# Weighting the first half's attention groups at the operand loads of the out-projection, in a hybrid decoder layer on one core

## The chip, the core and the metric

The kernel runs on one core of a Trainium2 chip. The metric is the device time of one execution in microseconds (us), lower is better. Engines are named as in the profile: PE (TensorE matmul), PEld (its weight load), DVE (VectorE), ACT (ScalarE), POOL (GpSimd), SP (SyncE). In this kernel POOL does hardly more than issue DMAs, and SP does nothing else. Each engine takes its own instructions in order; semaphores hold one back until what it reads is there.

## The reference

One layer over 2048 tokens of width 1024, in float32. Three mixers run side by side on slices of one projection; the concatenation of their outputs goes through an out-projection, and an MLP follows. What the change touches is the end of the attention mixer: three groups of two heads each give an output o and a log-sum-exp, and a softmax over the groups weights the outputs.

```python
h = rmsnorm(x, norm1_g)
z = h @ w_in                          # q|k|v, conv a|gate, LRU gate|x
for g, (window, dilation) in enumerate(((128, 1), (512, 4), (2048, 16))):
    o, lse = dilated_window_attention(q_g, k_g, v_g, ...)   # 2 heads of 64
alpha = softmax(stack(lse), axis=groups)
y_attn = o * alpha[..., None]         # 6 heads = 384 channels
mix = concat([y_attn, conv_module(...), recurrent_mixer(...)])
x = x + mix @ w_out
x = x + relu(rmsnorm(x) @ w_up) ** 2 @ w_down
return rmsnorm(x, final_g)
```

## The kernel before

Channels lie on partitions, tokens along the free axis. The 2048 tokens are worked in two halves of 1024 (h = 0, 1), each in two blocks of 512 (m = 0, 1). A matmul's operands are split into a rounded high part and a low rest, and each product is three matmuls (high·high, high·low, low·high), so every operand costs one ACT copy (high) and one DVE subtraction (low): `split` (L242, L243) and `halves` (L907, L908).

The stages: `inproj(0)`; `inproj(1)` with the first half's mixers between its steps; then for each half the out-projection, the up product and the down product, with the second half's mixers spread through the first half's stages by `tick`. A scheduler orders the instructions of the first part by priority and readiness: `mixers(0)` is recorded with a raised priority and so lands among the instructions of `inproj(1)`. Its parts are attention, the convolution, the recurrent mixer (`lru_mixer`, three passes t = 0, 1, 2) and `combine`.

In `inproj`, one group of 48 matmuls takes 10.9 us into two of four PSUM banks (`mm`); DVE empties them (L388, L390, L393) while PE fills the other two. Weights come by SP into five `raw` tiles (L251) and are split by L242 and L243 some groups ahead.

A pass of `lru_mixer` loads x (`wide<-lscr`, L542) and gate weights (`mr<-gates_w`, L543), runs four steps of a short convolution on DVE (L548, then L552 three times), splits the result (L242 and L243 into `wr`), and multiplies it on PE by the gate weights into bank `cb` (L564 to L566). ACT applies the sigmoid (L567), and DVE and ACT go on with L569, L573 to L580, the scan (L582) and L586; L588 stores to `mscr`. PE's gate matmuls stand among those of `inproj` in one order, so PE waits at L564 or L565 if `wr` is late.

`combine(h)` gets per-token maxima and sums of each group from `sscr` (L802, to `m`), forms the three weights (L808 to L823, small DVE operations and one ACT exponential), and stores them to `wscr` (L827). Then for each of six tiles (block b, group g) it loads the weights back, each row repeated on 64 partitions (L841, two DMAs of 128 KB), loads the group's output from `oscr` (L843), multiplies (L834, 128x512) and stores to `mscr` (L850, L854). For h = 0 all its DMAs go through SP, for h = 1 through POOL.

The out-projection reads eight 128-channel tiles per block from `mscr`: `act_load` (L922) loads some of them into the lower halves of `rounded` tiles, `act_split` (L924) splits them. `MIX_ORDER = [3, 4, 5, 6, 7, 0, 1, 2]` puts attention's three tiles last (n = 5, 6, 7), loaded by one DMA. For the first half `out_first` brings in block 1 during the last groups of `inproj(1)`, `out_second` block 0 afterwards. The matmuls are L948 to L950, 24 to a group of one bank; groups 0 to 3 read block 1, groups 4 to 7 block 0.

Small tiles of 512 columns (`mtile`, `m`) come from a ring of 15, shared by attention, `combine` and the recurrent mixer of the second half.

Of the kernel before, what the change touches and what calls it, by code (L numbers as in the profile page):

```python
# [16 lines left out]
NB = 512  # L17
KT = D // P
F = 4096
HD = 64  # L20
# [14 lines left out]
MIX_ORDER = [3, 4, 5, 6, 7, 0, 1, 2]  # L35
# [44 lines left out]
def body(tc, xt, w_in, w_v, w_out, w_up, w_down, vecs, lru_wa, lru_wx, consts, g_row, out, out_rows):  # L80
    nc = tc.nc
# [26 lines left out]
    def X(i):  # L108
        return rounded[i // 4][:, i % 4 * HS:(i % 4 + 1) * HS]
# [25 lines left out]
    def mtile():  # L135
        return mp.tile([P, 544], F32, name="m", tag="M")
# [30 lines left out]
    oscr = tc.dram_tile([3, P, S], F32, name="oscr")  # L167
    sscr = tc.dram_tile([3, S, 4], F32, name="sscr")
    rscr = tc.dram_tile([S], F32, name="rscr")
    wscr = tc.dram_tile([3, 2, S], F32, name="wscr")  # L170
# [282 lines left out]
    def loads(h):  # L453
        return nc.gpsimd if h else nc.sync

    def stores(h):
        return nc.gpsimd if h else nc.sync
# [335 lines left out]
    def combine(h):  # L793
        t0 = h * HS
        ml = mtile()
        both = ml[:, 128:320].rearrange("p (g w f) -> p g w f", g=3, f=4)
        m = ml[:, 0:48].rearrange("p (g w) -> p g w", g=3)
        l = ml[:, 48:96].rearrange("p (g w) -> p g w", g=3)
        top, tot = ml[:, 96:112], ml[:, 112:128]
        for j in range(2):  # L800
            for g in range(3):
                loads(h).dma_start(both[j * HD:(j + 1) * HD, g], sscr[g][t0:t0 + HS].rearrange("(c w) f -> c w f", w=16))  # L802
        yield 0
        yield 0
        yield 0
        for j in range(2):
            jp = slice(j * HD, (j + 1) * HD)
            nc.vector.tensor_copy(m[jp], both[jp, :, :, j])  # L808
            nc.vector.tensor_copy(l[jp], both[jp, :, :, 2 + j])

        def wide(a):
            return a.unsqueeze(1).to_broadcast([P, 3, 16])

        nc.vector.tensor_max(top, m[:, 0, :], m[:, 1, :])
        nc.vector.tensor_max(top, top, m[:, 2, :])
        nc.vector.tensor_tensor(m, m, wide(top), OP.subtract)
        nc.scalar.activation(m, m, AF.Exp)
        yield 1.2
        nc.vector.tensor_tensor(l, l, m, OP.mult)
        nc.vector.tensor_add(tot, l[:, 0, :], l[:, 1, :])  # L820
        nc.vector.tensor_add(tot, tot, l[:, 2, :])
        nc.vector.reciprocal(tot, tot)
        nc.vector.tensor_tensor(m, m, wide(tot), OP.mult)  # L823
        yield 1.2
        for g in range(3):
            for j in range(2):
                stores(h).dma_start(wscr[g][j, t0:t0 + HS].rearrange("(c w) -> c w", w=16), m[j * HD:(j + 1) * HD, g, :])  # L827
        yield 0
        parts = [(b, g) for b in range(2) for g in range(3)]
        held = []  # L830

        def scale():
            c, g, w, o = held.pop(0)
            nc.vector.tensor_mul(o, o, w)  # L834
            return c, g, o

        for b, g in parts:
            c = slice(t0 + b * NB, t0 + (b + 1) * NB)
            w = mtile()[:, :NB]
            for j in range(2):  # L840
                loads(h).dma_start(w[j * HD:(j + 1) * HD, :], wscr[g][j:j + 1, c].to_broadcast([HD, NB]))  # L841
            o = mtile()[:, :NB]
            loads(h).dma_start(o, oscr[g][:, c])  # L843
            held.append((c, g, w, o))
            yield 0
            yield 0
            if len(held) == 3:
                c, g, o = scale()
                yield 0.7
                stores(h).dma_start(mscr[g][:, c], o)  # L850
        while held:
            c, g, o = scale()
            yield 0.7
            stores(h).dma_start(mscr[g][:, c], o)  # L854

    def mixers(h):
        if h:
            yield from attention(h)
            yield from combine(h)
            yield from conv_rest(HS)  # L860
            yield from lru_mixer(h)
        else:
            yield from attention(0)
            yield from conv_whole(0, HS, True)
            yield from lru_mixer(0)
            yield from combine(0)
# [30 lines left out]
    def hi(i):  # L897
        return X(i)[:, :NB]

    def lo(i):  # L900
        return X(i)[:, NB:]

    def f32(a):
        return a.bitcast(F32)

    def halves(raw, h, l):
        nc.scalar.copy(h, raw)  # L907
        nc.vector.tensor_sub(l, raw, f32(h))  # L908
# [3 lines left out]
    ACTS = (16, 8)  # L912
    CHANNELS = (0, 4, 1, 5, 2, 6, 3, 7)

    def out_at(n):
        return 1 - n // 4 % 2, n % 4 + n // 8 * 4

    def act_load(h, m, n0, n1):
        i, t0 = ACTS[m] + n0, h * HS + m * NB
        k = MIX_ORDER[n0]  # L920
        dst = rounded[i // 4].rearrange("p (s b n) -> p s b n", s=4, b=2)[:, i % 4:i % 4 + n1 - n0, 1, :]
        nc.sync.dma_start(f32(dst), mscr[k:k + n1 - n0, :, t0:t0 + NB].rearrange("k p n -> p k n"))  # L922

    def act_split(m, n):  # L924
        i = ACTS[m] + n
        halves(f32(lo(i)), hi(i), lo(i))

    def out_pair(w, pairs):
        if w in (2, 3):
# [22 lines left out]
    def out_first(pairs):  # L952
        out_load(0, pairs)
        out_load(1, pairs)
        for n0, n1 in ((0, 2), (2, 4), (4, 5), (5, 8)):
            act_load(0, 1, n0, n1)
        last_act = next(i for i in reversed(nc.cur_bb.bb.instructions) if i.engine == mybir.EngineType.Activation)
        with tc.issue_after(last_act):
            out_split(0, pairs)
            for n in range(KT):  # L960
                act_split(1, n)

    def out_second(h, pairs):
        if not h:
            out_load(2, pairs)
            out_load(3, pairs)
        for n0, n1 in ((0, 2), (2, 4), (4, 5), (5, 8)):
            act_load(h, 0, n0, n1)
# [64 lines left out]
    def outproj(h, wts, banks, begun):  # L1033
# [50 lines left out]
        for n in range(16):  # L1084
# [7 lines left out]
            if 1 <= n < 4:  # L1092
                for i in range(*((0, 3), (3, 6), (6, 8))[n - 1]):
                    act_split(0, i)
# [526 lines left out]
    for h in range(2):  # L1621
# [10 lines left out]
        def hooks(kp):  # L1632
            if kp == 0:
                while aside[0] is not None:
                    tick(1e9)
            elif h == 0 and kp == 1:
                close("early0")
                nb = pool("xb1", 1, reuse_waits="tile")
                rounded[6] = nb.tile([P, 4 * HS], F32R, name="rounded7")
                state_["pairs"] = left_pairs(1)  # L1640
            elif h == 0 and kp == 2:
                out_load(0, state_["pairs"])
            elif h == 0:
                for n0, n1 in ((), ((0, 2),), ((2, 4),), ((4, 5), (5, 6)), ((6, 8),), ())[kp - 2]:
                    act_load(1, 1, n0, n1)
                if kp in (3, 5, 6):
                    out_load({3: 1, 5: 2, 6: 3}[kp], state_["pairs"])
                if kp > 3:
                    act_split(1, 2 * kp - 8)
                    act_split(1, 2 * kp - 7)  # L1650
                if kp == 5:
                    out_split(0, state_["pairs"])
# [67 lines left out]
```

## Time and profile before

| what | value |
|---|---|
| time, median of 3 runs | 2002.42 us |
| lowest and highest of these runs | 2000.58 and 2003.43 us |
| the profiled execution | 1999.48 us, span 1997.7 us |
| PE's mean granted clock | 0.996 |
| DMA issues on SP between 300 and 375 us: `m<-wscr`, `m<-oscr`, `mscr<-m` | 12, 6, 6 |

The span runs from the first to the last instruction of the profiled execution; the 1.8 us between it and that execution's time lie around it. Times in views count from the span's start. In a list of instructions a row gives start, duration, engine, line, operation, output tile <- input tiles, shape and count (neighbours of one kind are merged); the bracket says how long the engine had idled before it and what ended that. The half's mixers lie between about 60 and 440 us, the first half's out-projection begins at 509 us.

### The profile page before, as it was taken

To read this page: it belongs to the slowest core of one execution; us is meant where nothing else is said; L and a number is where in the kernel's file an instruction comes from. 1 tells how busy PE (TensorE), PEld (TensorE's weight loads), DVE (VectorE), ACT (ScalarE), POOL (GpSimd) and SP (SyncE) were. 2 spreads that over 40 slices of the span, in tenths; PEclk is the share of its full clock that TensorE was granted. 3 is DMA by queue.
4 is the path that set the end of the run, shared out by engine and by line. 5 is a ranking of instruction groups with operands and counts; after the bars stand their busy time and mean duration, and the time that the engine had idled before them with its cause. 6 is when DMAs were issued, how large, how long until landed. Compare 5 with 4: busy or idle time off the path is not lost.

```text
span 1997.7 us, 25490 instructions
## 1 busy us (share of the span) xinstructions
PE 1956.4 (98%) x8906; PEld 1593.7 (80%) x8906; DVE 1450.5 (73%) x1976; ACT 1050.4 (53%) x1634; POOL 168.2 (8%) x297
## 2 busy tenths in 40 slices
PE   8999998999999999999999999999999999999998
PEld 6887776789777777888888878788888888888886
DVE  7899785794567665887969899867555555577884
ACT  6144875513556764556656566446545555444343
POOL 0023200000022423000000000100000000000001
PEclk9999999999999999999999999999999999999999
DMA  5555596635555646544788777764444447786773
GB/s 169 165 151 159 165 294 196 216 121 165 182 168 164 196 151 217 193 154 162 271 286 279 249 275 248 245 199 146 158 153 151 145 143 262 240 293 215 263 260 136
DMA packets 202124, 399.78 MB, mean 200 GB/s; under 512 B 25382, under 2 KB 33814, under 8 KB 201932
## 3 DMA queue, kind: packets, MB, share of 16 engines
q1 hardware_dynamic: 182548, 342.02, 51.0%
q0 software_dynamic: 16096, 45.38, 7.8%
q10 hardware_dynamic: 3352, 10.76, 1.6%
q8 instruction: 70, 1.15, 0.2%
q14 instruction: 58, 0.48, 0.1%
HBM read 287.47 MB, written 119.00 MB: 203 GB/s over the span
## 4 chain that ended last, share of the span: by engine, by line
PE 82%; DVE 7%; DMA 5%; ACT 3%; issue 2%; SPq 0%; POOL 0%; DVEq 0%; ACTq 0%
PE bank L1135 10%; PE bank L1136 10%; PE bank L1137 10%; PE bank L1497 8%; PE bank L1498 8%; PE bank L1499 8%; PE mm L265 4%; PE mm L262 4%; PE mm L268 4%; PE bank L948 2%; PE bank L949 2%; PE bank L950 2%; DVE wide L474 1%; PE mm L425 1%; PE mm L427 1%
## 5 line engine op out<-in xcount | busy, mean ns | idle before, releaser
L1135 PE MATMUL bank<-rounded,pair 128*128 128x512 f32 x896 | 353.1, 394 | 2.8 <-ACT low L1144 2.2
L1136 PE MATMUL bank<-rounded,pair 128*128 128x512 f32 x896 | 351.7, 393 | 0.0
L1137 PE MATMUL bank<-rounded,pair 128*128 128x512 f32 x896 | 351.3, 392 | 0.0
L1497 PE MATMUL bank<-rounded,rounded 128*128 128x512 f32 x688 | 268.3, 390 | 1.7 <-DVE z L1510 1.4
L1499 PE MATMUL bank<-rounded,rounded 128*128 128x512 f32 x688 | 268.1, 390 | 0.0
L1498 PE MATMUL bank<-rounded,rounded 128*128 128x512 f32 x688 | 268.1, 390 | 0.0
L908 DVE TENSOR_TENSOR rounded<-rounded 128x1024 fp32r<-128x1024 f32 (+1 forms) x172 | 186.5, 1097 | 74.7 <-ACT rounded L907 73.6
L907 ACT CAST rounded<-rounded 128x1024 fp32r<-128x1024 f32 (+1 forms) x172 | 160.9, 949 | 134.5 <-DMA rounded<-fscr 102.8
L1135 PEld LDWEIGHTS bank<-rounded,pair 128*128 128x128 f32 x896 | 168.8, 188 | 41.5 <-ACT low L1144 2.6
L1137 PEld LDWEIGHTS bank<-rounded,pair 128*128 128x128 f32 x896 | 168.4, 188 | 35.9
L1136 PEld LDWEIGHTS bank<-rounded,pair 128*128 128x128 f32 x896 | 168.6, 188 | 34.9 <-issue 0.2
L262 PE MATMUL mm<-rounded,rounded 128*128 128x512 f32 x496 | 159.5, 397 | 8.4 <-ACT rounded L242 7.1
L268 PE MATMUL mm<-rounded,rounded 128*128 128x512 f32 x496 | 159.1, 396 | 0.0
L265 PE MATMUL mm<-rounded,rounded 128*128 128x512 f32 x496 | 157.4, 394 | 0.0
L907 ACT CAST rounded<-kept 128x1024 fp32r<-128x1024 f32 x80 | 84.1, 1051 | 133.7 <-DVE kept L1307 66.1
L1497 PEld LDWEIGHTS bank<-rounded,rounded 128*128 128x128 f32 x688 | 129.2, 188 | 29.3 <-DVE z L1510 1.8
L1499 PEld LDWEIGHTS bank<-rounded,rounded 128*128 128x128 f32 x688 | 129.2, 188 | 27.4 <-DVE rounded L908 0.4
L1498 PEld LDWEIGHTS bank<-rounded,rounded 128*128 128x128 f32 x688 | 129.2, 188 | 26.7
L242 ACT CAST rounded<-raw 128x512 fp32r<-128x512 f32 (+1 forms) x96 | 55.6, 582 | 146.8 <-PE mm L265 92.7
L907 ACT CAST pair<-wraw 128x1024 fp32r<-128x1024 f32 x64 | 67.1, 1048 | 117.1 <-PE bank L1136 111.2
L908 DVE TENSOR_TENSOR rounded<-kept,rounded 128x1024 fp32r<-128x1024 f32 x80 | 97.8, 1222 | 39.6 <-ACT rounded L907 39.3
L908 DVE TENSOR_TENSOR pair<-wraw,pair 128x1024 fp32r<-128x1024 f32 x64 | 78.2, 1222 | 60.6 <-ACT pair L907 60.5
(371 smaller groups left out, 3727.4 us busy)
## 6 DMA issues: line engine op xcount, KB each, us to landing
fscr<-low SPq DMA_DIRECT2D x224, 256.0 KB, 2.1
rounded<-fscr SPq DMA_DIRECT2D x112, 512.0 KB, 4.2
second<-in_w_down SPq DMA_DIRECT2D x80, 512.0 KB, 5.7
kept<-in_w_down SPq DMA_DIRECT2D x48, 512.0 KB, 5.4
raw<-in_w_in SPq DMA_DIRECT2D x64, 256.0 KB, 4.0
low<-in_w_up SPq DMA_DIRECT2D x64, 256.0 KB, 3.1
wraw<-in_w_up SPq DMA_DIRECT2D x64, 256.0 KB, 3.0
raw<-in_xt SPq DMA_DIRECT2D x32, 256.0 KB, 3.5
```

The costliest lines, as they stand in the source:

```text
L242: nc.scalar.copy(h, raw)
L262: nc.tensor.matmul(bank, wh[:, sl], ah[:, cols], start=first_, stop=False)
L265: nc.tensor.matmul(bank, wh[:, sl], al[:, cols], start=False, stop=False)
L268: nc.tensor.matmul(bank, wl[:, sl], ah[:, cols], start=False, stop=last_)
L907: nc.scalar.copy(h, raw)
L908: nc.vector.tensor_sub(l, raw, f32(h))
L1135: nc.tensor.matmul(bank, wh[:, sl], hi(x), start=fresh and k == 0, stop=False, **kw)
L1136: nc.tensor.matmul(bank, wh[:, sl], lo(x), start=False, stop=False, **kw)
L1137: nc.tensor.matmul(bank, wl[:, sl], hi(x), start=False, stop=k == KH - 1, **kw)
L1497: nc.tensor.matmul(banks[j], th[:, c], sh[:, x], start=fresh and k0, stop=False, **kw)
L1498: nc.tensor.matmul(banks[j], th[:, c], sl[:, x], start=False, stop=False, **kw)
L1499: nc.tensor.matmul(banks[j], tl[:, c], sh[:, x], start=False, stop=k1, **kw)
```

## The change

For h = 0, `combine` now ends after storing the weights to `wscr`: the loop of six tiles that loads, multiplies and stores is not run. Instead `act_load` for the first half loads each of attention's three tiles of a block by itself, straight from `oscr` into the lower half of its `rounded` tile (SP), and the weights, repeated on 64 partitions, into an `m` tile of its own by two DMAs on POOL; `act_split` multiplies the two into the `m` tile (DVE) and splits that. The other five tiles come from `mscr` as before. The second half is unchanged: its `combine` runs whole, between the steps of the up product.

```diff
@@ combine
             for j in range(2):
                 stores(h).dma_start(wscr[g][j, t0:t0 + HS].rearrange("(c w) -> c w", w=16), m[j * HD:(j + 1) * HD, g, :])
         yield 0
+        if h == 0:
+            return
         parts = [(b, g) for b in range(2) for g in range(3)]
@@
+    shares = {}
+
     def act_load(h, m, n0, n1):
         i, t0 = ACTS[m] + n0, h * HS + m * NB
         k = MIX_ORDER[n0]
+        if h == 0 and k < 3:
+            for n in range(n0, n1):
+                g = MIX_ORDER[n]
+                nc.sync.dma_start(f32(lo(ACTS[m] + n)), oscr[g][:, t0:t0 + NB])
+                w = shares[m, n] = mtile()[:, :NB]
+                for j in range(2):
+                    nc.gpsimd.dma_start(w[j * HD:(j + 1) * HD, :], wscr[g][j:j + 1, t0:t0 + NB].to_broadcast([HD, NB]))
+            return
         dst = rounded[i // 4].rearrange("p (s b n) -> p s b n", s=4, b=2)[:, i % 4:i % 4 + n1 - n0, 1, :]
         nc.sync.dma_start(f32(dst), mscr[k:k + n1 - n0, :, t0:t0 + NB].rearrange("k p n -> p k n"))
 
     def act_split(m, n):
         i = ACTS[m] + n
-        halves(f32(lo(i)), hi(i), lo(i))
+        x = f32(lo(i))
+        if (m, n) in shares:
+            w = shares.pop((m, n))
+            nc.vector.tensor_mul(w, w, x)
+            x = w
+        halves(x, hi(i), lo(i))
```

In the changed program the load from `oscr` is L928, the broadcast L931 and the product L941; lines between `combine` and `act_load` stand 2 further down, those after `act_split` 17.

The scheduler reorders around it. The first place is the start of the recurrent mixer's second pass, some 325 us into the span. SP's queue there, before the change (`raw` are weight loads of the in-projection, `m<-sscr` the sums for the weights, `wide<-lscr` the second pass's x):

```order
L251 DMA raw_99<-in_w_in 128x512
L802 DMA m<-sscr 64x64 x6
L571 DMA wide<-gscr 128x1024
L251 DMA raw_100<-in_w_in 128x512
L827 DMA wscr<-m 64x16 x2
L542 DMA wide<-lscr 128x1027
L827 DMA wscr<-m 64x16 x4
```

And with it:

```order
L251 DMA raw_99<-in_w_in 128x512
L928 DMA rounded_80<-oscr 128x512
L802 DMA m<-sscr 64x64 x5
L571 DMA wide<-gscr 128x1024
L802 DMA m<-sscr 64x64
L251 DMA raw_100<-in_w_in 128x512
L542 DMA wide<-lscr 128x1027
L399 DMA uscr<-z 128x1024
```

A load of an attention output has come in ahead of the sums, the stores of the weights (L827) have gone from this place, and the load of x follows the weight load at once.

DVE at the same place before (L816 is the step ahead of the exponential, `z<-mm` empties a bank):

```order
L816 TENSOR_TENSOR m<-m 128x48
L819 TENSOR_TENSOR m<-m 128x48
L820 TENSOR_TENSOR m<-m 128x16
L821 TENSOR_TENSOR m<-m 128x16
L822 RECIPROCAL m<-m 128x16
L823 TENSOR_TENSOR m<-m 128x48
L569 TENSOR_TENSOR wide<-wide 128x1024
L393 TENSOR_TENSOR z<-mm,row_105 128x512 x2
L395 TENSOR_TENSOR z<-z 128x512 x2
L243 TENSOR_TENSOR rounded_83<-raw_101,rounded_83 128x512
L548 TENSOR_SCALAR wide<-wide,vec 128x1024
```

And with the change:

```order
L816 TENSOR_TENSOR m<-m 128x48
L548 TENSOR_SCALAR wide<-wide,vec 128x1024
L569 TENSOR_TENSOR wide<-wide 128x1024
L393 TENSOR_TENSOR z<-mm,row_105 128x512 x2
L395 TENSOR_TENSOR z<-z 128x512 x2
L243 TENSOR_TENSOR rounded_83<-raw_101,rounded_83 128x512
L577 SCALAR_TENSOR_TENSOR wide<-wide 128x1024
L552 SCALAR_TENSOR_TENSOR wide<-wide,vec 128x1024
L819 TENSOR_TENSOR m<-m 128x48
L552 SCALAR_TENSOR_TENSOR wide<-wide,vec 128x1024
L820 TENSOR_TENSOR m<-m 128x16
```

The steps that finish the weights (L819 on) have moved behind the start of the pass, and L548, which reads the load of x, stands first.

The second place is where the products stand, some 345 to 360 us into the span. DVE before:

```order
L586 TENSOR_TENSOR wide<-wide 128x1024
L243 TENSOR_TENSOR wr<-wide,wr 128x512
L834 TENSOR_TENSOR m<-m 128x512 x3
L243 TENSOR_TENSOR rounded_83<-raw_99,rounded_83 128x512
L243 TENSOR_TENSOR wr<-wide,wr 128x512
L834 TENSOR_TENSOR m<-m 128x512
L390 TENSOR_TENSOR z<-mm,row_105 128x512 x2
L243 TENSOR_TENSOR rounded_83<-raw_100,rounded_83 128x512
L548 TENSOR_SCALAR wide<-wide,vec 128x1024
```

And with the change:

```order
L243 TENSOR_TENSOR wr<-wide,wr 128x512
L821 TENSOR_TENSOR m<-m 128x16
L822 RECIPROCAL m<-m 128x16
L823 TENSOR_TENSOR m<-m 128x48
L243 TENSOR_TENSOR rounded_83<-raw_99,rounded_83 128x512
L243 TENSOR_TENSOR wr<-wide,wr 128x512
L941 TENSOR_TENSOR m<-m,rounded_80 128x512 x2
L390 TENSOR_TENSOR z<-mm,row_105 128x512 x2
L243 TENSOR_TENSOR rounded_83<-raw_100,rounded_83 128x512
L548 TENSOR_SCALAR wide<-wide,vec 128x1024
L941 TENSOR_TENSOR m<-m,rounded_80 128x512
L569 TENSOR_TENSOR wide<-wide 128x1024
```

Where four of the six old products stood, the last three steps of the weights and the three new products of block 1 now stand, with two instructions between the weights and the first product. The other two old products stood behind the L552 that follows (before L580); nothing stands there now. The products of block 0 stand among the operand splits at the end of `inproj(1)`.

POOL's broadcasts for these products, with the loads of the second half's attention around them (L656 a bias, L603 and L612 queries and keys, L622 values); before, only the latter stood there:

```order
L931 DMA m<-wscr 64x512 x5
L656 DMA m<-in_consts 128x512
L603 DMA m<-zscr 64x2x256
L931 DMA m<-wscr 64x512
L603 DMA m<-zscr 64x2x256
L612 DMA mr<-zscr 64x384 x4
L622 DMA m<-vscr 128x3x128
L931 DMA m<-wscr 64x512 x6
```

The six of block 1 stand ahead of and between these loads, the six of block 0 behind the first values.

## The prediction

> **What bounds the kernel now.** I read the first part of the page, then the chain that ended last, then the list of what PE waited for, then the stages one by one.
>
> ```profile
> span 1997.7 us, 25490 instructions
> ...
> PE 1956.4 (98%) x8906; PEld 1593.7 (80%) x8906; DVE 1450.5 (73%) x1976; ACT 1050.4 (53%) x1634; POOL 168.2 (8%) x297
> ...
> PE 82%; DVE 7%; DMA 5%; ACT 3%; issue 2%; SPq 0%; POOL 0%; DVEq 0%; ACTq 0%
> ```
>
> PE is busy 98% of the span, so work moved between other engines is worth only what it adds to or takes from PE's 41 us of waiting. In the list of PE's waits (total, times, longest) I look for those that name a tile of the stage where the change lies:
>
> ```profile
> PE cb L565 <- DVE state L584: 1.9, 1, 1.9
> PE mm L425 <- DVE z L393: 1.8, 1, 1.8
> PE cb L564 <- ACT wr L242: 1.7, 2, 0.9
> ```
>
> Busy time by stage (PE first, DVE third, then PE's clock and the DMA share) shows where they fall:
>
> ```profile
> 325.00:350.00 25.00, 24.15 (x106) 19.49 (x106) 20.55 (x31) 14.94 (x17) 1.67 (x3) 1.00 0.78 220
> 350.00:375.00 25.00, 22.24 (x95) 17.23 (x94) 19.16 (x23) 14.18 (x16) 2.21 (x5) 1.00 0.80 259
> 375.00:400.00 25.00, 25.00 (x109) 20.05 (x108) 17.61 (x19) 13.79 (x16) 0.00 (x0) 1.00 0.50 178
> 500.00:525.00 25.00, 25.00 (x113) 20.58 (x112) 12.94 (x23) 11.15 (x18) 0.00 (x0) 1.00 0.55 180
> ```
>
> From 325 to 375 us, where the old combination ran between the steps of the recurrent mixer, PE lost 3.6 us, always to the gate matmuls (L564, L565), which stand in PE's order and need operands that DVE makes. Around 500 to 525, where the out-projection starts and where the change is meant to act, PE lost nothing. So the change is decided at 325 to 375, by DVE's order.
>
> **What is removed and added, and what is hidden.** Gone from SP: 12 broadcast loads, 6 loads and 6 stores of the combination, and two 3-tile loads; added: 6 loads on SP and 12 on POOL. SP's queue is not what PE waits for here, so I count this at nothing; if a weight load were late instead, PE would wait, but raw tiles are loaded five deep. Six multiplications L834 of 128x512 become six of the same size. Three of them (tokens 512 to 1023) stay in the in-projection stage, as the order shows; three move to the operand splits:
>
> ```profile
> 504.48 1.90 DVE L908 TENSOR_TENSOR rounded<-rounded 128x512 fp32r<-128x512 f32 x3 [0.28 <-ACT rounded L907]
> 509.11 0.47 PE L948 MATMUL bank<-rounded,pair 128*128 128x512 f32 x1
> 530.19 1.21 POOL L603 DMA_DIRECT2D m<-zscr  x2 [63.36 <-PE cb L721]
> ```
>
> The last splits end at 506.4, and those of the three moved tiles are first read by the fifth group of 24 matmuls, at 0.23 us a matmul some 22 us after 509.11. Three multiplications (1.9 us) fit there. The six broadcasts of these tiles stand on POOL behind the second half's first loads and hold its next ones back some 3 us; POOL idled 63 us after those, until 530: nothing.
>
> **Term 1: the recurrent mixer's second pass.** In DVE's new order L548 stands ahead of L569; it waits for its load L542, which SP issues behind L251. Before:
>
> ```profile
> 324.29 0.34 SPq L251 DMA_DIRECT2D raw<-in_w_in  x1
> 328.84 0.58 SPq L542 DMA_DIRECT2D wide<-lscr  x1
> 326.50 0.21 DVE L819 TENSOR_TENSOR m<-m 128x48 f32<-128x48 f32 x1 [1.24 <-ACT m L817]
> 328.50 1.23 DVE L569 TENSOR_TENSOR wide<-wide 128x1024 f32<-128x1024 f32 x1 [0.84 <-ACT wide L567]
> 330.06 1.29 DVE L393 TENSOR_TENSOR z<-mm,row 128x512 f32<-128x512 f32 x2 [0.33 <-PE mm L268]
> 333.06 0.81 DVE L548 TENSOR_SCALAR wide<-wide,vec 128x1024 f32<-128x1024 f32 x1
> 342.55 1.28 DVE L388 SCALAR_TENSOR_TENSOR z<-mm,row 128x512 f32<-128x512 f32 x2
> 343.34 0.50 PE L564 MATMUL cb<-wr,mr 128*128 128x512 f32 x1 [0.85 <-ACT wr L242]
> DMA to landing us min/median/max: 5.1/7.2/8.0
> ```
>
> The last row is L542's landing over its issues; the one at 328.84 landed in at most 4.2 (L548 at 333.06 did not wait), with little in flight. The new issue, 324.65, follows a weight load at once; I take 5.1, so L548 starts at 329.75. From L569 to L388 the old chain took 342.55 - 328.50 = 14.05. Without the 0.33 idle and with L819 and the still shorter L820 now inside it (some 0.4 together) it is 14.1, L548 included. It ends at 343.85 instead of 342.55: **+1.3**, and L564 with it. Bounds: a landing too early to matter leaves L569 waiting for ACT (some 329.3): +0.1; a landing of 8.0: +4.2.
>
> **Term 2: the weights.** The new order puts L821 to L823 behind DVE's L243 that follows L586, then two L243, then the first two multiplications. So the weights are stored, broadcast and used within a few DVE instructions.
>
> ```profile
> 345.54 0.69 DVE L243 TENSOR_TENSOR wr<-wide,wr 128x512 fp32r<-128x512 f32 x1
> 351.63 0.69 DVE L243 TENSOR_TENSOR wr<-wide,wr 128x512 fp32r<-128x512 f32 x1 [1.06 <-ACT wr L242]
> 356.27 1.29 DVE L390 TENSOR_TENSOR z<-mm,row 128x512 f32<-128x512 f32 x2 [2.78 <-PE mm L268]
> 359.64 0.81 DVE L548 TENSOR_SCALAR wide<-wide,vec 128x1024 f32<-128x1024 f32 x1 [1.49 <-issue]
> 366.98 1.29 DVE L834 TENSOR_TENSOR m<-m 128x512 f32<-128x512 f32 x2
> 351.98 0.38 SPq L542 DMA_DIRECT2D wide<-lscr  x1
> 329.46 2.36 SPq L827 DMA_DIRECT2D wscr<-m  x4
> wscr<-m SPq DMA_DIRECT2D x6, 4.0 KB, 2.8
> m<-wscr POOLq DMA_DIRECT2D x12, 128.0 KB, 6.3
> DMA to landing us min/median/max: 2.7/6.2/7.8
> ```
>
> With +1.3 the first L243 ends at 347.45 and L823 (three operations of L819's size, some 0.7 together) at 348.15. The stores go out 0.59 apart, the fourth at 349.9; landed 2.8 later, 352.7; its broadcast, issued then, lands 6.3 later, the second half's figure for the same transfer on POOL: 359.0. DVE is free from 353.6, so it waits 5.4 us in all at the two multiplications, and ends them at 359.7. Behind them stand L390, L243, L548, the third multiplication, then L569 to L552; for none of the first three does PE wait yet, since the banks and split weights are a group of 10.9 us ahead. L390 starts 3.4 late; with L243 it takes 1.8. But the old order idled 1.49 before L548 (its load, issued 351.98, landed 7.6 later). So L548 starts at 361.5, the third multiplication (some 0.6) ends at 362.9, and the rest, as long as before from the end of L548 to the L834 (366.98 - 360.45 = 6.5), at 369.4, against 366.98: **+2.4** at that point, term 1 included. Bounds: landing of 2.7 (the shortest of L841, last row) and term 1 at +0.1: +0.6; of 7.8 and term 1 at +4.2: +6.8.
>
> **Term 3: what comes back.** The two L834 at 366.98 (1.2 us) are gone behind it.
>
> ```profile
> 367.77 0.50 PE L564 MATMUL cb<-wr,mr 128*128 128x512 f32 x1 [0.89 <-ACT wr L242]
> 368.19 1.22 DVE L580 TENSOR_TENSOR wide<-wide 128x1024 f32<-128x1024 f32 x1
> 369.32 2.03 DVE L388 SCALAR_TENSOR_TENSOR z<-mm,row 128x512 f32<-128x512 f32 x2
> 373.97 0.67 DVE L243 TENSOR_TENSOR wr<-wide,wr 128x512 fp32r<-128x512 f32 x1
> 374.70 0.50 PE L565 MATMUL cb<-wr,mr 128*128 128x512 f32 x1 [1.87 <-DVE state L584]
> 384.57 2.03 DVE L390 TENSOR_TENSOR z<-mm,row 128x512 f32<-128x512 f32 x2 [4.20 <-PE mm L268]
> ```
>
> L564 goes to 370.2. L388 reads the bank that PE closes just behind it, at 371.2 (DVE alone would be there at 370.5), so only 0.4 of the 1.2 comes back: L243 ends 5.24 after 371.3, and L565 starts at 376.7 against 374.70: **+2.0**. At 384.57 DVE waits for PE (4.20 idle), so the delay passes on whole, and PE never idled from 375 to 400. The sum is 1999.48 + 2.0 = 2001.5 for the profiled execution (span 1997.7 plus 1.8 around it). That execution lies 2.9 under the median of the runs shown, 2002.42; in those terms I forecast **2004.4**.
>
> The clock bears on this.
>
> ```profile
> 443.25 0.44 PE L425 MATMUL mm<-rounded,rounded 128*128 128x384 f32 x1 [1.79 <-DVE z L393]
> 425.00:450.00 25.00, 23.21 (x104) 20.06 (x103) 20.85 (x22) 5.43 (x9) 0.00 (x0) 0.93 0.36 123
> ```
>
> In the stage of the 1.79 us wait the granted clock was 0.93: 0.07 of 25 us, 1.7 us, were lost besides the wait. In the stage of the 1.87 at 374.70 it stayed at 1.00. The waits near 343 and 370 become 2 us and more, so one more such dip is possible; before 376.7 DVE is later than PE anyway and hides most of it, behind it the sum would be +3.7. The Trainium skill's page "TensorE: Matmul & The Clock Gate", "Part 1: The HAM clock gate", has the clock halved only after an idle window of about 3.4 us; by that the sum stays +2.0. The row at 443.25 speaks against trusting it.
>
> **The rivals.**
> Slower, by one mechanism: L542's load at 324.65 lands late among the weight and gate loads. Each microsecond beyond 5.1 is one on L564 at 344 and on all behind it. From 7.1 on the total passes +4, that is 0.2%; at 8.0 it is +4.9, with a slow broadcast or a dip +6.5 to +8: 2007 to 2010. For it: 7.6 at 351.98; against: at most 4.2 at 328.84.
> Faster: the shift changes how DVE stands to PE, and a wait elsewhere goes, the 1.79 at 443.25 with its dip (3.5 together) and some of the 0.9 and 1.9 here: -4 to -5, some 1998. Against: DVE's order from 384 to 443 is unchanged and starts from PE.
> The broadcast is quick, 2.7 as in the shortest row: the second product waits until 355.4 only, L390 starts with PE at 357.6, L548 when its load lands at 360.9, and L565 comes at 376.1: +1.4, 2003.8. The Trainium skill's page "DMA: Bandwidth & Descriptors", section "Anatomy of one DMA — SWDGE (gpsimd) path", speaks for it: it fits a POOL-issued DMA as 2.0 us plus bytes over 436 GB/s, an estimate of 2.3 us for these 128 KB; the medians of 6.2 and 6.3 in the rows speak against.
> The change doesn't do what it says for half its tiles: their weighting stays among the mixer's steps. That is in the order and so in my sum; did it not matter, the time would be that of before, 2002.4.
>
> **How the numbers follow.** The case as worked, +0.2 to +4: 0.50; quick broadcast: 0.12; no effect: 0.08; these three lie within 0.2%. Late load, past +4: 0.21; the faster rival: 0.09. About 0.2%, 4 us, is what a measurement of this kernel can tell from no change. The terms' bounds put the sum between about 0 and +6.5, and the runs of before lie 1.8 below to 1.0 above their median: I give 2000.0 to 2009.0. The main case alone: 2002 to 2006.5.
>
> **What would show it.** Right: L548 near 330 waiting for its load; DVE idle about 5 us ahead of the first two products at 354 to 360; PE's waits at L564 of about 2.5 and 2, and a shorter one than 1.87 at L565; from 400 us on every row about 2 us later; no wait of PE at 500 to 525. Wrong: a wait of L948 on the moved products, or of L262 on weights; L548 starting before 328; DVE not idle at 354.

## The result and the profile after

The changed kernel takes 2010.89 us (median of 7 runs, 2007.83 to 2018.08), the one before 2002.42 (7 runs, 1999.54 to 2004.54): a ratio of 1.0053, with a 95% interval of 1.0041 to 1.0066. In a second comparison (the first experiment below) the ratio was 1.0035 (1.0023 to 1.0048). A ratio here is not the quotient of the two medians; these differ by 8.5 and 6.6 us. So the change costs 0.35% to 0.53%, where the forecast was 2 us in a range up to 2009.0.

The first part of the page and the chain that ended last, after the change:

```profile
span 2015.9 us, 25479 instructions
...
PE 1963.1 (97%) x8906; PEld 1597.1 (79%) x8906; DVE 1450.8 (72%) x1976; ACT 1051.5 (52%) x1634; POOL 174.5 (9%) x309
...
PE 71%; DMA 11%; DVE 9%; ACT 5%; issue 4%; SPq 0%; POOL 0%; DVEq 0%; ACTq 0%; POOLq 0%
```

PE's instructions are as many as before, but they take 6.7 us longer (1963.1 against 1956.4), so beside more waiting there is slower running. What PE waited for (total, times, longest), the rows that name a tile of the stage:

```profile
PE cb L564 <- ACT wr L242: 8.9, 2, 6.4
...
PE mm L425 <- DVE z L393: 2.0, 1, 2.0
...
PE bank L965 <- DVE z L393: 1.2, 1, 1.2
```

The gate matmul L564 waits 8.9 us instead of 1.7, L565 no longer 1.9, and a wait is new: L965, the out-projection's first line. Busy time by stage, PE first, the granted clock third from the end:

```profile
325.00:350.00 25.00, 22.47 (x96) 17.66 (x95) 18.61 (x30) 14.92 (x18) 0.00 (x0) 0.98 0.30 100
350.00:375.00 25.00, 23.97 (x98) 18.56 (x96) 9.98 (x16) 11.10 (x13) 6.97 (x13) 0.95 0.74 201
375.00:400.00 25.00, 19.65 (x78) 15.45 (x79) 17.56 (x20) 14.79 (x18) 0.00 (x0) 0.86 0.45 156
500.00:525.00 25.00, 23.83 (x106) 19.43 (x105) 17.41 (x27) 12.95 (x20) 4.05 (x7) 1.00 0.68 192
```

DVE is busy 10 of 25 us from 350 to 375, and from 350 to 400 the clock stood at 0.95 and 0.86: (0.05 + 0.14) x 25 = 4.75 us of full speed were withheld. About 2 of these lie in PE's wait from 373.97 to 380.35 us itself (granted clock 0.69 there, PE idle) and cost nothing more; the rest makes PE's matmuls slower. Where DVE stood shows the list of instructions of SP's queue, POOL, DVE and PE, in that order:

```profile
351.90 3.03 SPq L827 DMA_DIRECT2D wscr<-m  x5
357.21 0.33 SPq L251 DMA_DIRECT2D raw<-in_w_in  x1
357.59 0.43 SPq L571 DMA_DIRECT2D wide<-gscr  x1
358.06 0.45 SPq L827 DMA_DIRECT2D wscr<-m  x1
358.56 0.96 SPq L542 DMA_DIRECT2D wide<-lscr  x1
355.33 2.61 POOL L931 DMA_DIRECT2D m<-wscr  x5 [87.24 <-PE mm L268]
368.34 0.52 POOL L931 DMA_DIRECT2D m<-wscr  x1 [8.73 <-DMA wscr<-m]
359.73 0.69 DVE L941 TENSOR_TENSOR m<-m,rounded 128x512 f32<-128x512 f32 x1 [0.79 <-DMA m<-wscr]
362.12 0.69 DVE L941 TENSOR_TENSOR m<-m,rounded 128x512 f32<-128x512 f32 x1 [1.70 <-DMA m<-wscr]
369.12 0.87 DVE L548 TENSOR_SCALAR wide<-wide,vec 128x1024 f32<-128x1024 f32 x1 [4.34 <-DMA wide<-lscr]
372.35 0.69 DVE L941 TENSOR_TENSOR m<-m,rounded 128x512 f32<-128x512 f32 x1 [2.36 <-DMA m<-wscr]
380.35 0.80 PE L564 MATMUL cb<-wr,mr 128*128 128x512 f32 x1 [6.38 <-ACT wr L242]
```

The first two products stand about where they were forecast, counted from the first gate matmul. Then L548 waits 4.34 us for its load (issued 358.56, used 369.12, 10.6 us) and the third product 2.36 us for a broadcast that POOL could issue only at 368.34, since the sixth store, issued at 358.06, had not landed. PE's gate matmuls pay.

This execution lies 7 us above the kernel's median, and an early part of its surplus isn't the change's: PE's first L564 stands at 318.3 us here and at 315.0 in the first trace of before. So all traces below are read by three distances: from PE's first L564 to its last L425 (the **stretch**, the recurrent mixer and the rest of `inproj(1)`), from there to the out-projection's first matmul (the **step**), and from there to the end. The rows for the stretch, grouped by line, after the change:

```profile
L564 PE MATMUL cb<-wr,mr x12: 392/500/795, 318.3 to 393.3; 128*128 128x512 f32 x12
L425 PE MATMUL mm<-rounded,rounded x128: 331/334/525, 79.7 to 487.4; 128*128 128x384 f32 x128
```

487.4 - 318.3 = 169.1 us; before, 475.9 - 315.0 = 160.9.

### The profile page after: what moved, and what is told of

Its sections match the earlier page's. It is cut to its first block, busy times and chain, and to the rows that moved or that the text cites. A ratio compares the mean times of both kernels' runs of the same rounds, so it can differ in the third digit from the quotient of the medians.

```text
span 2015.9 us, 25479 instructions
## 1 busy us (share of the span) xinstructions
PE 1963.1 (97%) x8906; PEld 1597.1 (79%) x8906; DVE 1450.8 (72%) x1976; ACT 1051.5 (52%) x1634; POOL 174.5 (9%) x309
## 4 chain that ended last, share of the span: by engine, by line
PE 71%; DMA 11%; DVE 9%; ACT 5%; issue 4%; SPq 0%; POOL 0%; DVEq 0%; ACTq 0%; POOLq 0%
PE bank L1152 9%; PE bank L1153 9%; PE bank L1154 9%; PE bank L1516 7%; PE bank L1514 7%; PE bank L1515 7%; PE mm L265 3%; PE mm L262 3%; PE mm L268 3%; PE bank L966 2%; PE bank L965 2%; PE bank L967 2%; DMA raw<-in_xt 2%; DMA rounded<-fscr 1%; DMA second<-in_w_down 1%
## 5 line engine op out<-in xcount | busy, mean ns | idle before, releaser
L262 PE MATMUL mm<-rounded,rounded 128*128 128x512 f32 x496 | 160.8, 400 | 8.8 <-ACT rounded L242 7.5
```

The source lines that it names most:

```text
L262: nc.tensor.matmul(bank, wh[:, sl], ah[:, cols], start=first_, stop=False)
```

## The experiments

Times are medians beside those of the kernel before on the same chip; the interval is that of the ratio. Stretch and step are from each run's trace, as differences of rounded starts, so they are good to 0.1 us.

| kernel | time, before (us) | ratio (95%) | stretch | step |
|---|---|---|---|---|
| before, two traces | | | 160.9, 159.3 | 33.2, 33.3 |
| the change, four traces | 2007.91, 2001.36 | 1.0035 (1.0023 to 1.0048) | 169.1, 162.3, 168.4, 165.1 | 34.5, 34.2, 34.7, 34.5 |
| products held back, two traces | 2004.12, 2001.36 | 1.0013 (1.0001 to 1.0026) | 163.9, 163.0 | 34.5, 34.7 |
| no weighting | 1999.77, 2001.36 | 0.9995 (0.9984 to 1.0006) | 159.1 | 33.3 |
| block 0 alone | 2003.82, 2001.36 | 1.0012 (1.0000 to 1.0025) | 158.5 | 33.3 |
| block 1 alone | 2004.82, 2000.62 | 1.0032 (1.0020 to 1.0044) | 166.2 | 33.2 |
| own buffers | 2001.84, 2000.62 | 1.0008 (0.9996 to 1.0021) | 159.0 | 33.3 |
| three stores | 2008.05, 2000.62 | 1.0035 (1.0023 to 1.0048) | 163.9 | 34.7 |
| stores on POOL | 2005.28, 2000.62 | 1.0022 (1.0014 to 1.0031) | 160.8 | 34.8 |
| products behind the taps | 2006.55, 1998.78 | 1.0038 (1.0024 to 1.0052) | 163.3 | 34.4 |
| combination early | 2007.63, 2001.35 | 1.0029 (1.0018 to 1.0041) | 163.4 | 34.3 |
| early, products held back | 2008.32, 2001.35 | 1.0025 (1.0011 to 1.0039) | 162.7 | 34.6 |
| broadcasts on SP | 2008.30, 2000.71 | 1.0033 (1.0019 to 1.0048) | 164.1 | 35.3 |
| broadcasts on SP, products held back | 2007.49, 2000.71 | 1.0029 (1.0016 to 1.0043) | 160.0 | 35.1 |

### Where the loss stands: the two kernels again

> The changed kernel once more, for a second trace of it. Three theories. A: the loss arises where DVE stands waiting at block 1's three products (and at the L548 behind them) in the LRU's second and third pass, and nowhere else. B: it arises at block 0, whose broadcasts make POOL and the m buffers wait and whose products stand among the out-projection's splits. C: it arises from what the change does to the queues and to DVE's order ahead of the products (the oscr loads on SP, L548 first, the stores of the weights earlier). All three: 2008 to 2012 us. A: from the LRU's first matmul to its last this trace loses 8 to 9 us on the one of before again, whatever it loses elsewhere; the first 300 us and the stages from 500 us on, where the first trace lost another 10, come out within 2 to 4 us.

> The change again, one look, for its spread: the first trace lost 8.2 us between the LRU's first matmul and the in-projection's last, the second 1.4, while the timed loss is 6.5 to 8.5. If the loss stands in this stretch: 3 to 8 us here. If those two traces mislead: less than 2, and the loss then lies in the stages behind, which the change does not touch.

> As the run before: 3 to 8 us between the LRU's first matmul and the in-projection's last, 1 to 1.5 more at L965.

> The kernel before the change, a second trace. If its waits in this stretch (0.85, 0.89, 1.87 and 1.79 us) are as steady as its times: 161 us from the LRU's first matmul to the in-projection's last within 1 us, as in the first trace (475.9 less 315.0). If they vary as those of the change do, differences of single traces of 2 to 3 us tell nothing.

The change's stretch is 166.2 us in the mean of four traces, before 160.1: **+6.1**; the step 34.5 against 33.25: **+1.2**; from the out-projection to the end 1490.3 against 1489.4. The stretch varies by 7 us with the change and by 1.6 without, so a single trace of a kernel below places it only roughly. The second trace alone (162.3) missed the 8 to 9 us that theory A gave it, and would have misled. Of the +6.1, waits of PE are 3.6 (10.9, 7.0, 10.4 and 7.6 us against 5.4 and 5.3), and slower running 2.5 (PE busy 158.2, 155.3, 158.0 and 157.5 us against 155.5 and 154.0). The first L564 stands at 318.3, 316.6, 316.7 and 315.4 us against 315.0 and 315.8; whether that 1.4 us (in the mean) belongs to the change isn't settled, since the kernels below scatter from 314.5 to 320.0.

### Which part: one block alone, or the products left out

```diff
@@ only block 0 (for block 1 alone: b == 0, m == 1)
-        if h == 0:
-            return
-        parts = [(b, g) for b in range(2) for g in range(3)]
+        parts = [(b, g) for b in range(2) for g in range(3) if h or b == 1]
...
-        if h == 0 and k < 3:
+        if h == 0 and k < 3 and m == 0:
```

> Block 0 is weighted where the out-projection loads it, block 1 in the mixer's combination as before the change (three multiplications L836 and their loads stay in the combination). A: no product waits in the LRU by way of POOL's broadcasts; the combination's own three multiplications can wait for theirs, less: 2001 to 2005 us. B: the whole loss stays: 2008 to 2012. C: between, since only three of the six oscr loads are left where the change puts them: 2004 to 2008.

> Block 1 is weighted where the out-projection loads it, block 0 in the mixer's combination as before. If block 1 alone makes the loss: 2005 to 2010 us, with the waits in the LRU's third pass and the wait at L965 near 513 us both there. If block 0 makes a part of it: 2002 to 2005.

Block 1 alone has the whole loss in the stretch (166.2, ratio 1.0032), block 0 alone none (158.5). The wait at L965 needs both: block 1 alone has a step of 33.2.

For the next kernel the lines that broadcast the weights and put them into `shares` are deleted, so it leaves the first half's attention outputs unweighted.

> Leaves the weighting of the first half out: no broadcasts and no products for either block; the weights are still computed and stored, and the attention's groups are loaded from oscr as in the change. A: 2001 to 2004 us, within 2 us of the kernel that holds the products back. B: 2001 to 2004 as well, but then the kernel that holds them stays at 2009 or more. C: 2008 to 2011, as in the change.

Without products and broadcasts the stretch is 159.1 and the step 33.3, though L548 still stands first in the second pass. So theory C falls: neither the `oscr` loads nor the new order ahead of the products costs anything by itself that the time shows. It also shows the floor: even weighting nothing, the change would win nothing that can be measured.

```diff
@@ out_first: products held back
-        with tc.issue_after(last_act):
+        last_dve = next(i for i in reversed(nc.cur_bb.bb.instructions) if i.engine == mybir.EngineType.DVE)
+        with tc.issue_after(last_act), tc.issue_after(last_dve):
```

> The same work, but block 1's three products are held on DVE behind the in-projection's evacuation that is traced just before them, so they leave the LRU passes and stand at the operand splits before the out-projection. A: DVE no longer waits at the products, PE's waits at L564 of the second and third pass fall back from 2.5 and 6.4 to 1 to 2.5 us; only L548's place (some 1.7 us) is left: 2002 to 2005 us. B: block 0 is as in the change: 2009 to 2012. C: 2009 to 2012.

> The products held back, a second trace: L548 of the third pass waits 3 to 4 us for its load again, though no product stands ahead of it (broadcast traffic): the stretch takes 162 to 164 us. If that wait was chance: 159 to 161.

The time falls to 2004.12, within what theory A gave, but the stretch stays 3.4 above that of before. With the products held back, first trace (SP's queue, POOL, DVE, PE):

```profile
352.79 0.58 SPq L542 DMA_DIRECT2D wide<-lscr  x1
351.12 2.62 POOL L931 DMA_DIRECT2D m<-wscr  x5 [86.07 <-DMA wscr<-m]
353.72 0.57 POOL L656 DMA_DIRECT2D m<-in_consts  x1
357.13 1.29 DVE L390 TENSOR_TENSOR z<-mm,row 128x512 f32<-128x512 f32 x2 [3.95 <-PE mm L268]
362.98 0.82 DVE L548 TENSOR_SCALAR wide<-wide,vec 128x1024 f32<-128x1024 f32 x1 [3.96 <-DMA wide<-lscr]
371.11 0.50 PE L564 MATMUL cb<-wr,mr 128*128 128x512 f32 x1 [3.35 <-ACT wr L242]
```

No product stands ahead of L548 here, yet it waits 3.96 us, and 4.20 in the second trace: its load takes 10.2 us from issue to use. What is still there is POOL's traffic: the broadcasts from 351.12 us on and, right behind them, the bias load L656 of 256 KB. In POOL's order that load stands behind five of the broadcasts, and these wait for the weights; in the variants where no broadcast stands ahead of it, it goes out between 303 and 307 us. So this kernel doesn't tell the broadcasts from the bias load. The edit also shows why the products had moved: `issue_after` holds only instructions of the engine that it names, here ACT. The old splits begin on ACT, and their DVE half follows; a product begins on DVE, so nothing held it.

### The step: POOL and the m buffers

Second trace of the change, POOL, DVE and PE at the start of the out-projection:

```profile
498.76 1.20 POOL L603 DMA_DIRECT2D m<-zscr  x2 [29.84 <-DVE rounded L910]
499.96 2.09 POOL L612 DMA_DIRECT2D mr<-zscr  x4
509.36 0.69 DVE L941 TENSOR_TENSOR m<-m,rounded 128x512 f32<-128x512 f32 x1 [0.88 <-DMA rounded<-oscr]
511.71 2.48 DVE L393 TENSOR_TENSOR z<-mm,row 128x512 f32<-128x512 f32 x4
513.14 0.47 PE L965 MATMUL bank<-rounded,pair 128*128 128x512 f32 x1 [0.91 <-DVE z L393]
```

POOL's fetch for the second half's attention waits 29.84 us for an `m` buffer that a product holds until its split, goes out beside the out-projection's last loads, and DVE reaches L393 late. Before the change the same fetch went out at 462.8 us.

```diff
@@ own buffers: act_load, and between()
-                w = shares[m, n] = mtile()[:, :NB]
+                w = shares[m, n] = own[n] if m else mtile()[:, :NB]
...
             pairs.extend(left_pairs(0))
+            sp_ = pool("own", 1, reuse_waits="tile")
+            own.update({n: sp_.tile([P, NB], F32, name=f"own{n}") for n in range(KT) if MIX_ORDER[n] < 3})
...
```

> As the change, but block 1's three broadcasts go to buffers of their own, in the space that the LRU's wide tiles leave, instead of m buffers; their products come behind the LRU and hold no m buffer. Two theories of the part of the loss that stays when the products are held back (2.8 us there). D: in the change and in the kernel with held products, block 1's products sit in m buffers until their splits near 498 us; POOL's fetch of the attention's keys waits 28 to 30 us for these, goes out just when the out-projection's last operands are loaded, and delays them, so PE waits 0.9 to 1.2 us at L965 for DVE's L393. Then that wait goes here, POOL's L603 is not held until 498, and the time is 2000 to 2003 us. E: it comes from DVE's order in the second LRU pass (L548 first): 2003 to 2005, with PE still waiting at L965 or not.

With own buffers (POOL's bias load, then SP's queue, DVE, POOL, then DVE at the out-projection):

```profile
305.07 0.59 POOL L656 DMA_DIRECT2D m<-in_consts  x1 [38.15 <-PE mb L745]
354.46 0.58 SPq L542 DMA_DIRECT2D wide<-lscr  x1
360.61 0.81 DVE L548 TENSOR_SCALAR wide<-wide,vec 128x1024 f32<-128x1024 f32 x1
444.77 3.10 POOL L931 DMA_DIRECT2D own<-wscr  x6 [78.57 <-DMA cscr<-wide]
468.73 0.61 POOL L603 DMA_DIRECT2D m<-zscr  x1
508.33 2.65 DVE L393 TENSOR_TENSOR z<-mm,row 128x512 f32<-128x512 f32 x4 [0.73 <-PE mm L268]
```

The buffers come free only behind the mixer, so the broadcasts go out at 444.77. That takes the broadcasts, the products and the bias load out of the mixer's passes together. Both losses are gone: L548 doesn't wait (its load is there after at most 6.2 us), the fetch goes out at 468.73, DVE waits for PE at L393 and not the other way round; stretch 159.0, step 33.3, and the time can't be told from that of before. Theory D holds. None of the kernels tried is faster than the one before by more than the noise.

### Inside the stretch: which wait

```diff
@@ three stores: combine
+            if h == 0:
+                stores(h).dma_start(wscr[g][:, t0:t0 + HS].rearrange("j (c w) -> j c w", w=16), m[:, g, :])
+                continue
             for j in range(2):
@@ stores on POOL: combine
-                stores(h).dma_start(wscr[g][j, t0:t0 + HS].rearrange("(c w) -> c w", w=16), m[j * HD:(j + 1) * HD, g, :])
+                nc.gpsimd.dma_start(wscr[g][j, t0:t0 + HS].rearrange("(c w) -> c w", w=16), m[j * HD:(j + 1) * HD, g, :])
```

> As the change, but the first half's weights are stored by three transfers of both heads' rows instead of six, so that all of them are issued before the weight load L251 and the 512 KB load L571. If the late sixth store (6.5 to 10 us to land, where I took 2.8) is what made the wait at the third product: the sixth broadcast is issued with the others, the third product waits at most 2 us behind the second, and the time falls by 1 to 4 us, to 2004 to 2007. If what counts is the wait for the first broadcasts, or L548's own load: unchanged within 1 us, 2007 to 2009.

> As the change, but the first half's weights are stored by POOL's queue, just ahead of the broadcasts, so SP's queue is relieved of six issues (3.6 us) between its weight loads, and L251 is not held behind them. If SP's queue is a part of the loss: 2003 to 2006 us. If only the time from the weights to the products counts, and six issues on POOL cost as much as on SP: 2006 to 2009.

Three stores (POOL, DVE, PE; the added lines shift L931 to L934 and L941 to L944):

```profile
351.31 3.14 POOL L934 DMA_DIRECT2D m<-wscr  x6 [86.43 <-PE cb L566]
357.33 0.69 DVE L944 TENSOR_TENSOR m<-m,rounded 128x512 f32<-128x512 f32 x1 [4.25 <-DMA m<-wscr]
360.94 0.69 DVE L944 TENSOR_TENSOR m<-m,rounded 128x512 f32<-128x512 f32 x1 [2.91 <-DMA m<-wscr]
363.34 0.68 DVE L944 TENSOR_TENSOR m<-m,rounded 128x512 f32<-128x512 f32 x1
372.16 0.80 PE L564 MATMUL cb<-wr,mr 128*128 128x512 f32 x1 [3.81 <-ACT wr L242]
```

All six broadcasts go out together and the third product doesn't wait, but the first two now wait 4.25 and 2.91 us instead of 0.79 and 1.70, and the time stays: the late sixth store, which the profile of the change shows so plainly, isn't what the time hangs on. Stores on POOL fall between the change and the held products, with an interval that touches both, and a stretch (160.8) like that of before in its one trace; how much SP's queue matters stays open.

```diff
@@ products behind the taps: lru_mixer, act_split
+                    if h == 0:
+                        last_tap[0] = tap.ins
...
+            if m:
+                with tc.issue_after(last_tap[0]):
+                    nc.vector.tensor_mul(w, w, x)
...
```

> As the change, but block 1's three products are held on DVE behind the last convolution tap (L552) of the LRU's third pass: they stay in the LRU as work (1.9 us of DVE), but no longer stand ahead of L390 and L548 waiting for the broadcasts. If their waiting is what costs: as with the products held to the end, 2003 to 2006 us. If their work among the passes, or the broadcasts' traffic (which delays L548's own load), is what costs: 2007 to 2010.

It came out as slow as the change (1.0038), so the products' waiting for broadcasts isn't the whole cost: without it L548 waits for its load in its place (3.04 us), and the three products, 1.9 us of DVE's work, still stand in the pass ahead of what PE needs next.

```diff
@@ combination early: mixers
-            yield from combine(0)
+            with tc.high_priority(offset=1000):
+                yield from combine(0)
```

> As the change, but the first half's combination has a higher priority in the scheduler, so its steps stand together on DVE ahead of L569 again, as before the change, and the weights are stored near 330 instead of near 350 us; the products then stand in the second LRU pass. If the loss comes from the weights being 20 us late (broadcasts that collide with the loads L571 and L542 of the third pass, products that wait for them): PE's wait at L564 of the third pass is under 2 us, the stretch from the LRU's first matmul to the in-projection's last is 160 to 163 us, and the time is 2001 to 2005 us; what is left is the wait at L965 (1.2). If products anywhere in the LRU's passes cost this much: 2006 to 2010, with the wait moved to the second pass (the products at 335 to 340 waiting for broadcasts issued near 332).

> The combination early, as in the run before, and block 1's products held back to the splits before the out-projection: neither late broadcasts beside L571 and L542, nor products in the passes. If these two make the loss in the LRU: the stretch takes 159 to 161 us, as before the change, PE still waits about 1.2 us at L965, and the time is 2000 to 2003 us. If something else in the change costs: 2004 or more.

Both missed the faster time. With the combination early the products wait in the second pass, 0.55, 2.57 and 1.13 us (DVE, PE):

```profile
333.35 0.69 DVE L942 TENSOR_TENSOR m<-m,rounded 128x512 f32<-128x512 f32 x1 [0.55 <-DMA m<-wscr]
337.76 0.69 DVE L942 TENSOR_TENSOR m<-m,rounded 128x512 f32<-128x512 f32 x1 [2.57 <-DMA m<-wscr]
340.90 0.69 DVE L942 TENSOR_TENSOR m<-m,rounded 128x512 f32<-128x512 f32 x1 [1.13 <-DMA m<-wscr]
351.00 0.79 PE L564 MATMUL cb<-wr,mr 128*128 128x512 f32 x1 [5.01 <-ACT wr L242]
```

With the products held back as well, it is L548 of the second pass that waits (POOL, SP's queue, DVE, PE):

```profile
332.29 2.36 POOL L932 DMA_DIRECT2D m<-wscr  x4 [66.35 <-PE mm L265]
330.04 3.66 SPq L827 DMA_DIRECT2D wscr<-m  x6
333.75 0.58 SPq L542 DMA_DIRECT2D wide<-lscr  x1
339.94 0.81 DVE L548 TENSOR_SCALAR wide<-wide,vec 128x1024 f32<-128x1024 f32 x1 [2.88 <-DMA wide<-lscr]
347.03 0.50 PE L564 MATMUL cb<-wr,mr 128*128 128x512 f32 x1 [2.64 <-ACT wr L242]
```

So it isn't the lateness of the weights. Wherever they come, a pass gives way: x's load goes out late, behind the six stores on SP, or the products wait. Once issued, this load is there after 6.2 us, although four broadcasts go out within a microsecond and a half of it; the bias load goes out behind it, at 337.46 us.

Is it POOL's queue, beside SP's? The kernel before has the same broadcasts on SP, most of them issued behind x's load.

```diff
@@ broadcasts on SP: act_load
-                    nc.gpsimd.dma_start(w[j * HD:(j + 1) * HD, :], wscr[g][j:j + 1, t0:t0 + NB].to_broadcast([HD, NB]))
+                    (nc.sync if m else nc.gpsimd).dma_start(w[j * HD:(j + 1) * HD, :], wscr[g][j:j + 1, t0:t0 + NB].to_broadcast([HD, NB]))
```

> As the change, with block 1's broadcasts on SP's queue; the products stay in the passes. If POOL's queue is the cause: 2002 to 2005 us. If the bytes beside the load and the products in the passes are: 2006 to 2010, as the change.

> The products held back, and block 1's broadcasts on SP's queue instead of POOL's, five of them ahead of L571 and L542 in the order. If what delays L548's load is that a second queue (POOL's) runs beside SP's: the load lands within 8 us of its issue and the stretch is 159 to 161 us. If the bytes count wherever they are queued (the kernel before has the same broadcasts on SP, but spread out and mostly behind L542): L548 waits as long as with POOL, 3 to 4 us, and the stretch is 162 to 164. The wait at L965 stays in both: 2002 to 2004 against 2004 to 2007 us.

Neither is faster. With broadcasts on SP and products held back (SP's queue, DVE):

```profile
353.71 3.03 SPq L931 DMA_DIRECT2D m<-wscr  x5
356.79 0.58 SPq L571 DMA_DIRECT2D wide<-gscr  x1
357.41 0.43 SPq L542 DMA_DIRECT2D wide<-lscr  x1
364.95 0.81 DVE L548 TENSOR_SCALAR wide<-wide,vec 128x1024 f32<-128x1024 f32 x1 [3.71 <-DMA wide<-lscr]
```

The load now takes 7.5 us from issue to use, but it is issued 3 us later, behind the broadcasts, and L548 waits 3.71 us again. The time says what the held products on POOL's queue left unclear (1.0029 here, 1.0013 there; the intervals overlap): queueing the broadcasts elsewhere doesn't help. This trace's stretch of 160.0 is one execution with the clock at 1.00 from 325 to 400 us, 3.6 us under its kernel's median.

What the kernels have in common: with block 1's broadcasts ahead of or beside x's load of a pass, in either queue, L548 or a product waits and the ratio is 1.0013 to 1.0038; with those broadcasts behind the mixer, in the old combination or not there at all it is 0.9995 to 1.0012. By time alone the ends of the two groups (1.0013 and 1.0012) can't be told apart; the stretch is 160.0 to 169.1 in the first and 158.5 to 159.1 in the second. The bias load isn't what makes the groups: with the broadcasts on SP it goes out at 305.52 us, and the ratio is 1.0033.

## Why the prediction was wrong

**What bounds the kernel** was right in its first half: the loss was decided from 325 to 400 us by what DVE hands to PE's gate matmuls. "Around 500 to 525 ... PE lost nothing" held for before only.

**Term 1** was right: L564 of the second pass stands 28.4 us behind the first L564 before, and 30.0, 29.0, 29.5 and 29.6 after, +1.2 in the mean against +1.3, and L548 waits there for its load as forecast (5.13 us in the first trace). The close agreement is partly luck: own buffers and the second trace of the held products, with L548 first too, have 28.3 and 28.5. And the kernel without weighting, which has the same order, shows no loss by the end of the stretch: the mixer's later waits had room for it.

**Term 2 is the step that failed**, and in it not the part that I worked hardest on. The first two products end 44.5, 45.9, 44.6 and 45.2 us behind the first L564, against 44.7 forecast (359.7 - 314.98), though in the first trace DVE waited 4.62 us for ACT at the L243 ahead of them and only 2.49 at the products, where I had 5.4 at the products. What was mis-sized is what follows: "L548 starts at 361.5". I let DVE's order set L548, since its load had landed 7.6 us after its issue before, and did not price the load again with the broadcasts, and the bias load behind them, beside it. In the first trace it went out 40.2 us behind the first L564 instead of 37.0, behind a weight load that waited for DVE, and was used 10.6 us later. L548, forecast 46.5 us behind the first L564, came at 50.8, 47.6, 50.3 and 49.5; in the second trace it was not the load that held it but the products ahead of it, which waited 4.30 and 2.19 us. Held products and own buffers show the load by itself: 10.2 to 10.4 us from issue to use with POOL's traffic beside it, at most 6.2 without. L564 of the third pass, forecast 55.2 us behind the first (370.2), came at 62.0, 56.5, 61.2 and 58.3, and its wait was 6.38, 3.49, 6.20 and 4.67 us where I wrote "about 2". The late sixth store, which I had also priced at 2.8, was a miss of mine too, but the three stores show that it did not decide.

**The clock** was a mis-sized rider to it. I allowed one dip of 1.7 us, hidden; from 350 to 400 us the granted clock withheld 4.75, 1.75, 3.5 and 3.5 us in the four traces, of which 2.0, 0, 1.8 and 0.6 lie in PE's wait at L564 itself. I doubted the rule of the Trainium skill ("TensorE: Matmul & The Clock Gate", "Part 1: The HAM clock gate") that takes an idle window of about 3.4 us; with the products behind the taps, where PE's longest wait in the stretch is 2.44 us, the stages from 350 to 400 still show 0.96 and 0.97.

**Term 3** was right in kind (the wait at L565 is gone) but had no weight beside this.

**"Nothing" for POOL** was the second failure: 1.2 us. I looked at the fetch that idled until 530 us and took the one ahead of it for safe; but that one needs `m` buffers that block 1's products hold until their splits. I had named the queue that the broadcasts stand in and not the ring that they draw from.

**The rivals.** The slower one named the right kind of thing, a late load of x, in the wrong pass. The faster one did not come: L425's wait stays at 2.0.

**What stays open:** how the stretch's 6.1 us divide between the delayed load and the products. The held products suggest 3.4 for the load (two traces) and the rest for the products, but the other kernels with products held back are hardly faster than the change; they differ by less than their scatter. Open too is how much of the load's 10.2 to 10.4 us the bias load makes: no kernel has the broadcasts on POOL beside x's load of the third pass and the bias load early. With the bias load issued 7 us behind x's load (block 1 alone, where SP also carries block 0's old combination) the load still took 8.7.

## What to carry to other kernels

Work that is moved off an engine's busy place is only moved if something holds it there: look at which engine's instruction carries the hold, and whether the new first instruction is on that engine. Where a change puts several broadcasts beside a load that the critical pass waits for, price that load again, not the broadcasts alone, and look at what stands behind them in their queue and is held back with them. A buffer that lives longer has a next user in its ring; find it before counting a queue's wait as free.

## What was not expected of the hardware

The same 513.5 KB load of x of the third pass was used 9.2 to 11.3 us after its issue in the six traces where L548 waited for it with five of block 1's 128 KB broadcasts and the 256 KB bias load on POOL around it; 8.7 us after it with the broadcasts there and the bias load issued only 7 us behind it (block 1 alone); 7.4 and 7.5 us after it with five of the broadcasts ahead of it in its own queue and the bias load long gone; and at most 6.2 us after it without any of these.

A wait of some 2 us on PE does not always cost clock, not even in the same kernel: in the stage of the wait near 443 us the granted clock was 0.93 in the first trace of before (1.79 us, at 443.25) and 1.00 in its second (1.82 us, at 444.05); it was 1.00 with block 0 alone (2.00 us, at 444.01) and 0.93 with own buffers (2.01 us, at 442.21).
